# Five edits to the order of loads, sums and banks in a two-layer fp32 decoder kernel on one core

## The chip, the core and the metric

The kernel runs on one core of a Trainium2 chip. The metric is the device time of one launch in microseconds. Five engines work side by side, each with its own queue of instructions: TensorE (PE in the profile: matmuls and transposes), VectorE (DVE), ScalarE (ACT), GpSimd (POOL) and SyncE (SP), which in this kernel issues every DMA. Each engine takes its instructions in order, each as soon as what it waits for has come. One launch computes the whole trunk.

## The reference

The input x has 1024 rows of 1024 floats. Two layers each do

```
h = h + 0.5 * rmsnorm(swiglu(rmsnorm(h)))      first feed-forward, inner width 1408
h = h + rmsnorm(mixer(rmsnorm(h)))             layer 0: differential + gated linear attention
                                               layer 1: stick-breaking attention, 8 heads
h = h + 0.5 * rmsnorm(swiglu(rmsnorm(h)))      second feed-forward
```

with `swiglu(x) = (silu(x @ wg) * (x @ wu)) @ wd`. The mixers project their input (`hyb_w_in`, `sb_w_qkv`), attend causally and project back (`hyb_w_out`, `sb_w_out`). Everything is float32.

## The kernel before

**Products.** A float32 product is three matmuls in a faster format: each operand is split into a high and a low part, and `mm3` (L281 to L283) adds high·high, high·low and low·high into one PSUM bank. The high part is a copy on ScalarE (tile `hl` L271, for weights `wq` L330), the low part a subtraction on VectorE (L272, L331). So each operand, raw or summed, passes through ScalarE and VectorE before TensorE can use it. On top of that, large products are computed with fewer block products by sums and differences of blocks: the inputs' on VectorE (`combos`), the weights' on GpSimd (`rawt`/`t` L424 to L427 and `t` L64).

**Feed-forward.** `gu` has two phases over 11 column tiles c. Phase 1 multiplies the first half of the rows (A) with the gate weights (`pa`). In phase 1, after tile 2, `second_half()` transposes the other half of the rows (`xps` L321, copied to `xr` L323), and on tiles 3 to 6 `combos` builds the block sums that phase 2 needs, on VectorE. Phase 2 makes for each tile five quarter products into three banks: `pb`, `pc`, `pd`, then `pc` and `pd` once more, which are drained in between by adds on VectorE (L433, L436, L438). Then comes the down product: `da`, `db`, `dc`, `de`, and `dd` in two parts; between the parts of `dd` the epilogue adds to h, norms the first half of the rows and `make_x` (L250) transposes it for the next stage (`xps` L257).

**make_x** takes for the mixer a second output: a scaled copy of each transposed tile on ScalarE into `rawx`, and four DMAs that store these to `xkeep` in HBM.

**Mixer inputs.** `values()` (L738) computes the value rows by block products: `va`; then `vb` with the weights b21; then, after the second half's norm and transposes (`make_raw`, `xr`), `vc`, and on the same banks the products on S2, S1, S3, S4. The weight sums t1, t2, t4 (`T`, twelve operations, L64) and t3 are GpSimd's. The input differences are VectorE's: L800 to L802 for S2 and S1, L832 for S4. They need the raw first-half input K, which is loaded back from `xkeep` (four loads of `xk`).

**Heads.** `heads()` runs through units (head, block of 128 queries) in a pipeline; `start` is called on a head's first unit, `fill` on its fourth, and gives steps (the next head's projection, or `out_steps` in the last head) of which one is done per unit. In the stick-breaking mixer a unit's scores go through ScalarE (L1000, L1001), GpSimd (masks, L1004) and VectorE (a scan L1007, a product L1010) back to TensorE (`tps`). `out_weights` makes one of four sets of block sums of the output weights (loads, four GpSimd subtractions, four stores to `wsum`), at a head's start: in layer 1 one set for each of heads 0 to 3, in layer 0 two for each of heads 0 and 1. Before the last head the score pools are closed and opened again with two score banks and not four, so that `out_steps`, seven steps over four banks `oa`, has banks.

**What sets the order.** A scheduler takes the code and decides the order on each engine, with pools of buffers as limits: `raw` (name `rp`, four buffers, for everything that is loaded raw), `w`, `hl`, and eight PSUM banks. All loads and stores stand in SP's queue in one order, so a store that waits for GpSimd holds up each load behind it.

Of the kernel before, what the change touches and what calls it, by code (L numbers as in the profile page):

```python
# [87 lines left out]
class Trunk:  # L88
# [161 lines left out]
    def make_x(self, xns, gname, gi, pool, keep=None):  # L250

        nc = self.nc
        res = []
        for k in range(KD):
            ps = self.tp.tile([P, TB], F32, name="xps", tag="tp")
            for t in range(NTT):
                nc.tensor.transpose(ps[:, t * P:(t + 1) * P], xns[t][:, k * P:(k + 1) * P], self.ident)  # L257
# [86 lines left out]
    def gu(self, cx, wg, wu, A, xn1, gname, gi):  # L344
# [51 lines left out]
        for c in range(NF):  # L396
            h = [self.ph.tile([P, TB], F32, name="ph%d" % tb, tag="ph") for tb in range(2)]
            r = self.load_w(wg, c)
            w0, w1 = self.split_w(r[:, 0:4]), self.split_w(r[:, 4:8])
            ps = self.acc.tile([P, TB], F32, name="pa", tag="acc")  # L400
            self.quarter(ps, w0, A[0:4], True, True)
            nc.scalar.copy(out=h[1], in_=ps)
            if second:
                a12()
            second.append((ps, w1, h))
            ph.append(h)
            if c == 2:
                second_half()
            if 3 <= c <= 6:
                combos(c - 3)  # L410
# [7 lines left out]
        for c in range(NF):  # L418
# [11 lines left out]
            pd = self.acc.tile([P, TB], F32, name="pd", tag="acc")  # L430
            u2 = h[1]
            self.quarter(pb, self.split_w(t2), S[2], True, True)
# [5 lines left out]
            tt(out=c22, in0=pd, in1=c22, op=ALU.add)  # L438
            w4, w3 = self.split_w(b21), self.split_w(b22)
            self.quarter(pc, w4, A22, False, True)  # L440
            c21 = tm.tile([P, TB], F32, name="c21", tag="c21")
            tt(out=c21, in0=pc, in1=u2, op=ALU.add)
            nc.scalar.activation(out=c21, in_=c21, func=AF.Silu)
            self.quarter(pd, w3, S[4], False, True)
            c12 = tm.tile([P, TB], F32, name="c12", tag="c12")
            tt(out=c12, in0=pd, in1=u2, op=ALU.add)
# [143 lines left out]
    def down_strassen(self, w, ph, pg, hsrc, hdst, nxt):  # L590
# [127 lines left out]
        nxt0 = self.make_x(xns, *nxt, self.xp, self.xk if nxt[0] == "mix_pre_g" else None) if nxt else None  # L718
# [21 lines left out]
    def values(self, l, w, cols, X, xn1, vd):  # L740
# [25 lines left out]
        for t in range(NTT):  # L766
            nc.scalar.copy(out=p1[t], in_=pa[t])
        T = []
# [4 lines left out]
        self.rows_product(pb, A[4:8], weights(B.b21), True, 2)  # L773
# [5 lines left out]
        sp, kp = self.dyn(cv, "sx", 5), self.dyn(cv, "xk", KD // 2)  # L779
        kt = [kp.tile([P, 2, TB], F32, name="xk", tag="xk") for _ in range(KD // 2)]  # L780
        for k in range(KD // 2):
            nc.sync.dma_start(out=kt[k].rearrange("p k t -> p (k t)"), in_=self.xk[:, 2 * k * TB:2 * (k + 1) * TB])
        K = [kt[k // 2][:, k % 2] for k in range(KD)]
# [168 lines left out]
    def heads(self, H, first, second, third, fill, start):  # L952

        LAG = 2
        n = H * NQ
        pend, steps, last = [], [], None
        for u in range(n + LAG + 1):
# [24 lines left out]
            if old:  # L984
                last = old[:2] + (second(*old),)
            if done:
                third(*done)
        for step in steps:
            step()
# [23 lines left out]
    def sb_mixer(self, X):  # L1013
        a, nc = self.a, self.nc
        w = a["sb_w_qkv"][0]
        with ExitStack() as cx:
# [19 lines left out]
            def start(h):  # L1036
                if h == 7:
                    pd.close()
                    self.mctx.close()
                    self.open_mix(pd, 2, 1, 1)  # L1040
                if h % 2 and h < 7:
                    v[h // 2 + 1] = self.load_v(vp, self.vd, (h + 1) * P)
                if h < 4:
                    self.out_weights(1, h)

            def second(h, i, atts):
# [7 lines left out]
                if i == NQ - 1:  # L1054
# [3 lines left out]
                       lambda h: project(h + 1) if h < 7 else self.out_steps(1), start)  # L1058
# [195 lines left out]
    def hyb_mixer(self, X):  # L1254
# [3 lines left out]
        with ExitStack() as cx:  # L1258
# [81 lines left out]
            with ExitStack() as cd:  # L1340
# [9 lines left out]
                def start(h):  # L1350
                    if h == 3:
                        pd.close()
                        self.mctx.close()
                        self.open_mix(pd, 2, 1, 1)
                    if h == 1:
                        v[1] = self.load_v(vp, self.vd, 256)
                    if h < 2:
                        self.out_weights(0, 2 * h)
                        self.out_weights(0, 2 * h + 1)
# [10 lines left out]
                def fill(h):  # L1370
                    if h == 3:
# [5 lines left out]
                           third, fill, start)  # L1377
                pd.close()

    def put_o(self, l, k, ot, last=False):  # L1380
# [7 lines left out]
        if j >= 0:  # L1388
# [5 lines left out]
            self.out_sums(r, x, ot)  # L1394
            self.nc.sync.dma_start(out=self.sd[j][:, :S], in_=r)
            self.nc.sync.dma_start(out=self.sd[j][:, S:], in_=x)
# [19 lines left out]
    def out_weights(self, l, j):  # L1416
# [6 lines left out]
        B.sub(t[:, 0], r[:, 1], r[:, 0])  # L1423
        B.sub(t[:, 1], b[:, 1], r[:, 1])
        B.sub(r[:, 0], b[:, 1], t[:, 0])
        B.sub(b[:, 0], b[:, 0], r[:, 0])
        for i, src in ((0, t[:, 0]), (2, t[:, 1]), (1, r[:, 0]), (3, b[:, 0])):
            self.nc.sync.dma_start(out=self.td[j][:, i * TB:(i + 1) * TB], in_=src)

    def out_steps(self, l):  # L1430
# [10 lines left out]
        def step(n):  # L1441
            if n == 0:
                st["p1"] = halves([pair("p1") for _ in range(2)])
                st["c11"] = halves([pair("c11") for _ in range(2)])
                st["accs"] = self.new_accs("oa")
# [3 lines left out]
            a, b = self.split(r[:, 0], self.hp), self.split(r[:, 1], wp)  # L1449
            for t in range(NTT):  # L1450
                ts = slice(t * P, (t + 1) * P)
                self.mm3(st["accs"][t], a[:, 0, ts], a[:, 1, ts], b[:, 0], b[:, 1], n == 0, n in (3, 6), more=n > 3)
            if n in (3, 6):
                for t in range(NTT):
                    nc.scalar.copy(out=st["p1" if n == 3 else "c11"][t], in_=st["accs"][t])

        self.begun = B, order, st
        return [lambda n=n: step(n) for n in range(7)]
# [100 lines left out]
    def build(self):  # L1559
# [3 lines left out]
        self.xk = self.dram.tile([P, KD * TB], F32, name="xkeep")  # L1563
# [54 lines left out]
```

## Time and profile before

| | us |
|---|---|
| median of three runs | 2564.71 (2562.7 to 2566.6) |
| profiled execution, its own time | 2561.61 |
| its span | 2559.9 |
| TensorE busy | 2376.2 |
| VectorE busy | 1862.8 |
| ScalarE busy | 1173.6 |
| GpSimd busy | 945.3 |

The mean granted TensorE clock is 0.969 of full speed. TensorE's share is 93%; the rest is many short waits, the longest of 14 us, and after some of them the granted clock stands at half speed for a while. In the rows of the timeline the columns are start, duration, engine, line, operation, written tile<-read tiles, shapes and count, and in brackets the idle time before and what ended it. In the rows of the waits: who waited for what, total, times, longest. In the rows of windows: the window, its length, each engine's busy time with its number of instructions, the granted clock, the share of the DMA engines and GB/s.

### The profile page before, as it was taken

The page shows a single profiled execution, that of the slowest core. Times are in us where ns is not written, and L with a number is a line of the kernel's source. Part 1 is how long each engine was busy: PE and PEld are TensorE (multiplying, and loading weights), DVE is VectorE, ACT ScalarE, POOL GpSimd, SP SyncE. Part 2 cuts the span into 40 slices and gives each one's busy share as a digit, 9 for nine tenths or more (in the row PEclk, how much of TensorE's full clock was granted, in tenths as well). Part 3 has the DMA queues.
Part 4 walks back from the last instruction along what each step waited for, and adds up shares of the span by engine and source line. Part 5 has one row for each costly group of instructions (what it writes and reads, how often), then busy time and mean ns, then how long its engine had stood idle before and what let it go on. Part 6 is the DMA issues. An engine that isn't in the chain of part 4 may idle for free. (4 is left out here: it accounts for less than half of the span.)

```text
span 2559.9 us, 32090 instructions
## 1 busy us (share of the span) xinstructions
PE 2376.2 (93%) x11229; PEld 1937.5 (76%) x11229; DVE 1862.8 (73%) x2778; ACT 1173.6 (46%) x2335; POOL 945.3 (37%) x804
## 2 busy tenths in 40 slices
PE   7999977998999898999989999779899999899998
PEld 6887856777777777787868878558788887678876
DVE  6768866387577777767888678665676778686788
ACT  6423545332466667323465234444333345752343
POOL 2545423113211241555424454241332334234553
PEclk9999988999999999999999999889899999999999
DMA  5223554514311564223552225465321135622255
GB/s 162 82 80 97 179 179 159 173 46 136 115 58 58 169 201 124 83 75 115 165 185 83 83 70 198 157 205 163 125 83 58 50 120 166 192 83 71 73 157 197
DMA packets 272073, 318.49 MB, mean 124 GB/s; under 512 B 13780, under 2 KB 190120, under 8 KB 271912
## 3 DMA queue, kind: packets, MB, share of 16 engines
q1 hardware_dynamic: 271912, 316.45, 39.0%
q8 instruction: 88, 1.44, 0.2%
q14 instruction: 73, 0.60, 0.1%
HBM read 254.54 MB, written 61.87 MB: 124 GB/s over the span
## 5 line engine op out<-in xcount | busy, mean ns | idle before, releaser
L330 ACT CAST wq<-rawt 128x512 fp32r<-128x512 f32 x264 | 163.1, 623 | 355.5 <-PE pc L283 170.2
L225 POOL TENSOR_TENSOR rs<-ms,nhalf 128x1 f32<-128x1 f32 (+1 forms) x136 | 100.6, 745 | 427.4 <-DVE ms L223 374.3
L331 DVE TENSOR_TENSOR wq<-rawt,wq 128x512 fp32r<-128x512 f32 x264 | 239.2, 912 | 25.8 <-ACT wq L330 18.5
L424 POOL TENSOR_TENSOR rawt<-rawt 128x512 f32<-128x512 f32 x44 | 82.7, 1879 | 379.3 <-DMA rawt<-in_ffn_w_up_dram 136.8
L272 DVE TENSOR_TENSOR hl<-rawd,hl 128x512 fp32r<-128x512 f32 x168 | 150.8, 899 | 84.2 <-ACT hl L271 83.5
L281 PE MATMUL pps<-hl,wh 128*128 128x512 f32 x512 | 208.4, 407 | 0.0
L283 PE MATMUL pps<-hl,wl 128*128 128x512 f32 x512 | 202.5, 396 | 1.5 <-DVE wl L858 1.5
L282 PE MATMUL pps<-hl,wh 128*128 128x512 f32 x512 | 202.9, 396 | 0.0
L271 ACT CAST hl<-rawd 128x512 fp32r<-128x512 f32 x168 | 103.4, 619 | 186.6 <-PE dc L283 33.2
L281 PE MATMUL pd<-hl,wq 128*128 128x512 f32 x352 | 138.9, 395 | 10.7 <-DVE c L438 10.7
L281 PE MATMUL pc<-hl,wq 128*128 128x512 f32 x352 | 137.8, 392 | 6.6 <-DVE c L436 3.4
L281 PE MATMUL pa<-hl,wq 128*128 128x512 f32 x352 | 141.0, 401 | 3.1 <-DVE hl L275 3.1
L283 PE MATMUL pa<-hl,wq 128*128 128x512 f32 x352 | 139.8, 398 | 3.5 <-DVE wq L331 3.5
L282 PE MATMUL pa<-hl,wq 128*128 128x512 f32 x352 | 140.3, 399 | 0.0
L282 PE MATMUL pd<-hl,wq 128*128 128x512 f32 x352 | 138.8, 394 | 0.0
L283 PE MATMUL pd<-hl,wq 128*128 128x512 f32 x352 | 138.6, 394 | 0.0
L283 PE MATMUL pc<-hl,wq 128*128 128x512 f32 x352 | 138.3, 393 | 0.0
L282 PE MATMUL pc<-hl,wq 128*128 128x512 f32 x352 | 138.3, 393 | 0.0
L272 DVE TENSOR_TENSOR hl<-ph,hl 128x512 fp32r<-128x512 f32 x136 | 131.5, 981 | 0.0
L929 PE MATMUL z<-k,q 128*128 128x512 f32 (+2 forms) x480 | 124.3, 379 | 5.6 <-ACT e L1082 2.5
L1007 DVE TENSOR_TENSOR_SCAN a<-a,zero 128x128 f32<-128x128 f32 (+3 forms) x64 | 93.9, 1467 | 47.0 <-POOL a L1004 46.8
L283 PEld LDWEIGHTS pps<-hl,wl 128*128 128x128 f32 x512 | 96.6, 189 | 22.0 <-DVE wl L858 2.3
(343 smaller groups left out, 6885.5 us busy)
## 6 DMA issues: line engine op xcount, KB each, us to landing
rawt<-in_ffn_w_gate_dram SPq DMA_DIRECT2D x88, 512.0 KB, 4.0
rawd<-in_ffn_w_down_dram SPq DMA_DIRECT2D x60, 512.0 KB, 3.8
rawd<-in_ffn_w_down_dram SPq DMA_DIRECT2D x116, 256.0 KB, 2.8
rawt<-in_ffn_w_up_dram SPq DMA_DIRECT2D x44, 512.0 KB, 4.0
hres<-h SPq DMA_DIRECT2D x40, 512.0 KB, 2.9
h<-hres SPq DMA_DIRECT2D x40, 512.0 KB, 4.6
rawd<-in_hyb_w_in_dram SPq DMA_DIRECT2D x36, 256.0 KB, 3.5
rawd<-in_sb_w_qkv_dram SPq DMA_DIRECT2D x36, 256.0 KB, 3.5
```

The costliest lines, as they stand in the source:

```text
L225: nc.gpsimd.tensor_tensor(out=rs, in0=ms, in1=self.nhalf.to_broadcast([P, n]) if n > 1 else self.nhalf, op=ALU.pow)
L271: nc.scalar.copy(out=t[:, 0], in_=src)
L272: nc.vector.tensor_tensor(out=t[:, 1], in0=src, in1=t[:, 0].bitcast(F32), op=ALU.subtract)
L281: nc.tensor.matmul(ps, lhsT=ah, rhs=bh, start=first, stop=False, skip_group_check=more)
L282: nc.tensor.matmul(ps, lhsT=ah, rhs=bl, start=False, stop=False, skip_group_check=more)
L283: nc.tensor.matmul(ps, lhsT=al, rhs=bh, start=False, stop=last, skip_group_check=more)
L330: nc.scalar.copy(out=w[:, 0], in_=src)
L331: nc.vector.tensor_tensor(out=w[:, 1], in0=src, in1=w[:, 0].bitcast(F32), op=ALU.subtract)
L424: gt(out=b11, in0=b12, in1=b11, op=ALU.subtract)
L929: nc.tensor.matmul(z[:, :wide], lhsT=lhs[:, i * P:(i + 1) * P], rhs=rhs[:, c0:c0 + wide], start=j == 0, stop=j == len(passes) - 1 and not ...
L1007: nc.vector.tensor_tensor_scan(out=ra, data0=ra, data1=self.zero1.to_broadcast([P, n]), initial=1.0, op0=ALU.mult, op1=ALU.add)
```

## The change

Five things change.

1. `make_x` makes no raw copies and no stores. `values()` makes the raw inputs K itself, by eight additions of high and low part on GpSimd. In `values()` the weights b21 are loaded and split ahead of GpSimd's sums T.
2. In `gu`, `second_half()` comes after tile 3 and the combinations on tiles 4 to 7.
3. For the last tile of phase 2 the fourth and fifth quarter products have banks of their own, `pe` and `pf`.
4. `out_weights` and the sums of finished heads load first and put their GpSimd sums and stores into a list that runs one unit later. `out_weights` is called on unit 6 of heads 0 to 3 in layer 1, and on units 1 and 6 of heads 0 and 1 in layer 0.
5. The score pools keep four banks in the last head. `out_steps` takes two banks for two row tiles at a time: eight steps, four for each pair of row tiles; the operands are loaded and split in the first four and kept.

```diff
-    def make_x(self, xns, gname, gi, pool, keep=None):
+    def make_x(self, xns, gname, gi, pool):
...
-            if keep is not None:
-                if k % 2 == 0:
-                    r = self.rp.tile([P, 2, TB], F32, name="rawx", tag="raw")
-                nc.scalar.activation(out=r[:, k % 2], in_=ps, func=AF.Copy, scale=self.col(gname, gi * KD + k))
-                if k % 2:
-                    nc.sync.dma_start(out=keep[:, (k - 1) * TB:(k + 1) * TB], in_=r.rearrange("p k t -> p (k t)"))
...
-            if c == 2:
+            if c == 3:
                 second_half()
-            if 3 <= c <= 6:
-                combos(c - 3)
+            if 4 <= c <= 7:
+                combos(c - 4)
...
+            if last:
+                self.quarter(pe, self.split_w(b21), A22, True, True)
+                self.quarter(pf, self.split_w(b22), S[4], True, True)
+                tt(out=c12, in0=pd, in1=u2, op=ALU.add)
+                tt(out=c21, in0=pe, in1=c22, op=ALU.add)
+                tt(out=c22, in0=pd, in1=c22, op=ALU.add)
+                nc.scalar.activation(out=c21, in_=c21, func=AF.Silu)
+                tt(out=c12, in0=pf, in1=c12, op=ALU.add)
...
+        W = weights(B.b21)
         T = []
...
-        self.rows_product(pb, A[4:8], weights(B.b21), True, 2)
+        self.rows_product(pb, A[4:8], W, True, 2)
...
-        for k in range(KD // 2):
-            nc.sync.dma_start(out=kt[k].rearrange("p k t -> p (k t)"), in_=self.xk[:, 2 * k * TB:2 * (k + 1) * TB])
+        for k in range(KD):
+            gt(out=K[k], in0=A[k][:, 0].bitcast(F32), in1=A[k][:, 1].bitcast(F32), op=ALU.add)
...
+            soon, self.soon = self.soon, []
+            for f in soon:
+                f()
+            if u < n:
+                weights(h, i)
...
-                if h == 7:
-                    pd.close()
-                    self.mctx.close()
-                    self.open_mix(pd, 2, 1, 1)
...
-                if h < 4:
-                    self.out_weights(1, h)
...
+                       lambda h, i: self.out_weights(1, h) if h < 4 and i == 6 else None)
...
+                def weights(h, i):
+                    if h < 2 and i in (1, 6):
+                        self.out_weights(0, 2 * h + (i == 6))
...
+        self.soon.append(sums)
...
-        return [lambda n=n: step(n) for n in range(7)]
+        return [lambda tp=tp, ns=ns: step(tp, ns) for tp in range(2) for ns in ((0, 1), (2, 3), (4, 5), (6,))]
```

How the order moves is shown at three places of layer 0. The first is TensorE's queue between the two parts of `dd`, before (L257 is make_x's transpose, `fo_...` the normed row tiles, L281 to L283 the three matmuls of a product):

```order
L283 MATMUL dd_2642<-hl 128x512
L257 MATMUL xps<-ident,fo_1965 128x128 x4
L257 MATMUL xps<-ident,fo_1966 128x128 x4
L257 MATMUL xps<-ident,fo_1967 128x128 x4
L257 MATMUL xps<-ident,fo_1968 128x128 x4
L257 MATMUL xps<-ident,fo_1965 128x128
```

and after (here L256 is the transpose and L274 to L276 are the three matmuls):

```order
L274 MATMUL dd_2642<-hl 128x512
L256 MATMUL xps<-ident,fo_1967 128x128 x4
L274 MATMUL dd_2643<-hl 128x512
L275 MATMUL dd_2641<-hl 128x512
L276 MATMUL dd_2641<-hl 128x512
L274 MATMUL dd_2641<-hl 128x512
L256 MATMUL xps<-ident,fo_1968 128x128 x4
L275 MATMUL dd_2642<-hl 128x512
```

Before, 28 of the 32 transposes stand in one run ahead of the second part of `dd`; after, its matmuls stand between them. The second place is GpSimd's queue in `values()`, before:

```order
L64 TENSOR_TENSOR t_3349<-rawd 128x512
L64 TENSOR_TENSOR t_3350<-rawd,t_3349 128x512
L64 TENSOR_TENSOR t_3351<-rawd,t_3350 128x512
L64 TENSOR_TENSOR rawd<-rawd 128x512 x4
L819 TENSOR_TENSOR c_3777<-c_3777,p_3593 128x512
```

and after:

```order
L64 TENSOR_TENSOR t_3355<-rawd 128x512
L64 TENSOR_TENSOR t_3356<-rawd,t_3355 128x512
L64 TENSOR_TENSOR t_3357<-rawd,t_3356 128x512
L790 TENSOR_TENSOR xk<-hl 128x512 x8
L64 TENSOR_TENSOR rawd<-rawd 128x512 x4
```

The eight additions that make K stand behind the last of the twelve sums T and ahead of the sums t3. The third place is VectorE's queue behind `vb`, before (the numbered `t_...` are low halves of weight sums, `xr` of the second half's inputs, L800 the first difference with K):

```order
L775 TENSOR_TENSOR vo<-vb_3364,p_3308 128x512
L272 TENSOR_TENSOR hl<-t_3326,hl 128x512
L272 TENSOR_TENSOR hl<-xr,hl 128x512 x5
L800 TENSOR_TENSOR xk<-xk,xr 128x512
L272 TENSOR_TENSOR hl<-xr,hl 128x512
L801 TENSOR_TENSOR xr<-xr 128x512
```

and after (L265 are the low halves here, L807 the first difference with K):

```order
L783 TENSOR_TENSOR vo<-vb_3370,p_3294 128x512
L807 TENSOR_TENSOR xk<-xk,xr 128x512
L265 TENSOR_TENSOR hl<-t_3345,hl 128x512
L265 TENSOR_TENSOR hl<-xr,hl 128x512
L265 TENSOR_TENSOR hl<-t_3357,hl 128x512
L265 TENSOR_TENSOR hl<-xr,hl 128x512
```

The first difference with K (L807) now stands ahead of two of the four low halves that `vc` needs (`t_3345`, `t_3357`).

More of the change, by code (lines that the diff above doesn't have):

```diff
@@ L430, in gu @@
             pd = self.acc.tile([P, TB], F32, name="pd", tag="acc")
+            if c == NF - 1:
+                pe = self.acc.tile([P, TB], F32, name="pe", tag="acc")
+                pf = self.acc.tile([P, TB], F32, name="pf", tag="acc")
             u2 = h[1]
+            last = c == NF - 1
             self.quarter(pb, self.split_w(t2), S[2], True, True)
@@ L778, in values @@
         self.foctx.close()
[L779 to L783 removed]
+        sp, kp = self.dyn(cv, "sx", 5), self.dyn(cv, "xk", KD)
+        K = [kp.tile([P, TB], F32, name="xk", tag="xk") for k in range(KD)]
+        for k in range(KD):
+            gt(out=K[k], in0=A[k][:, 0].bitcast(F32), in1=A[k][:, 1].bitcast(F32), op=ALU.add)
         H = [None] * KD
@@ L950, in transposer, with heads @@
         return res, [lambda j0=j0: group(j0) for j0 in range(0, i + 1, 4)]
-    def heads(self, H, first, second, third, fill, start):
+    def heads(self, H, first, second, third, fill, start, weights):
         LAG = 2
@@ L987, in heads @@
                 third(*done)
-        for step in steps:
+        for step in steps + self.soon:
             step()
@@ L1393, in put_o, with sums @@
                 self.nc.sync.dma_start(out=ot, in_=self.ot[l][k])
-            self.out_sums(r, x, ot)
-            self.nc.sync.dma_start(out=self.sd[j][:, :S], in_=r)
-            self.nc.sync.dma_start(out=self.sd[j][:, S:], in_=x)
+            def sums():
+                self.out_sums(r, x, ot)
+                self.nc.sync.dma_start(out=self.sd[j][:, :S], in_=r)
+                self.nc.sync.dma_start(out=self.sd[j][:, S:], in_=x)
+            self.soon.append(sums)
     def out_order(self, l):
@@ L1421, in out_weights, with sums @@
         b = B.load((j + 4, 0), (j + 4, 1))
[L1423 to L1428, printed above, removed]
+        def sums():
+            B.sub(t[:, 0], r[:, 1], r[:, 0])
+            B.sub(t[:, 1], b[:, 1], r[:, 1])
+            B.sub(r[:, 0], b[:, 1], t[:, 0])
+            B.sub(b[:, 0], b[:, 0], r[:, 0])
+            for i, src in ((0, t[:, 0]), (2, t[:, 1]), (1, r[:, 0]), (3, b[:, 0])):
+                self.nc.sync.dma_start(out=self.td[j][:, i * TB:(i + 1) * TB], in_=src)
+        self.soon.append(sums)
     def out_steps(self, l):
@@ L1439, in out_steps, with load @@
         st = {}
-        def step(n):
+        ab = []
+        def load(n):
             if n == 0:
@@ L1448, in step @@
             nc.sync.dma_start(out=r[:, 1], in_=B.src(n, 0))
[L1449 to L1455, printed above, removed]
+            ab.append((self.split(r[:, 0], self.hp), self.split(r[:, 1], wp if n % 2 else self.xp)))
+        def step(tp, ns):
+            if 0 in ns:
+                st["accs"] = [self.acc.tile([P, TB], F32, name="oa%d" % t, tag="acc") for t in range(2)]
+            for n in ns:
+                if tp == 0:
+                    load(n)
+                a, b = ab[n]
+                for i in range(2):
+                    t = 2 * tp + i
+                    ts = slice(t * P, (t + 1) * P)
+                    self.mm3(st["accs"][i], a[:, 0, ts], a[:, 1, ts], b[:, 0], b[:, 1], n == 0, n in (3, 6),
+                             more=n > 3)
+                if n in (3, 6):
+                    for i in range(2):
+                        nc.scalar.copy(out=st["p1" if n == 3 else "c11"][2 * tp + i], in_=st["accs"][i])
         self.begun = B, order, st
-        return [lambda n=n: step(n) for n in range(7)]
+        return [lambda tp=tp, ns=ns: step(tp, ns) for tp in range(2) for ns in ((0, 1), (2, 3), (4, 5), (6,))]
     def mix_out(self, l, hsrc, hdst, gname, gi):
```

31 lines of the change are left out of this document (12 added, 19 removed).

## The prediction

> **What bounds the kernel now.** I read the page's busy times first, then the waits of TensorE, then the timeline around each long wait. TensorE is the bound:
>
> ```profile
> PE 2376.2 (93%) x11229; PEld 1937.5 (76%) x11229; DVE 1862.8 (73%) x2778; ACT 1173.6 (46%) x2335; POOL 945.3 (37%) x804
> PEclk9999988999999999999999999889899999999999
> ```
>
> The change takes no matmul out, so it can only win from TensorE's idle time (2559.9 - 2376.2 = 184 us, the modelled ends counted in) and from stretches where the granted clock is low. The waits of TensorE say where the idle time lies:
>
> ```profile
> PE vb L281 <- ACT hl L271: 27.3, 2, 14.0
> PE xps L257 <- DVE ms L223: 15.1, 9, 6.4
> PE dd L281 <- ACT hl L271: 14.0, 4, 6.6
> PE tps L945 <- DVE b L1010: 11.1, 1, 11.1
> PE pd L281 <- DVE c L438: 10.7, 4, 2.7
> PE xps L321 <- ACT fo L237: 9.9, 5, 2.3
> PE pc L281 <- DVE c L436: 3.4, 2, 1.7
> ```
>
> Each row is a place that one part of the change touches. The columns are total, times, longest. For every place the question is what comes late next once the wait is gone.
>
> **Part 1, the raw input tiles (make_x).** Before, the eight scaled copies into rawx and their four stores to xkeep stand in SP's queue ahead of the loads for dd's second product, and in TensorE's order all but four of the transposes stand ahead of that product. The change removes copies and stores, and the order then mixes that product with the transposes. The trace holds the same code without the stores: the end of layer 0's second feed-forward. The windows run from the last matmul ahead of the gap to the last of dd, over 106 matmuls each:
>
> ```profile
> core 0: us, PE busy (x) PEld busy (x) DVE busy (x) ACT busy (x) POOL busy (x), PEclk, DMA share, GB/s
> 333.60:377.30 43.70, 27.52 (x106) 20.07 (x105) 24.22 (x43) 23.72 (x45) 10.04 (x11) 0.73 0.50 169
> 1288.10:1313.60 25.50, 21.84 (x106) 16.36 (x106) 22.84 (x41) 16.92 (x35) 5.44 (x5) 1.00 0.66 207
> 1630.40:1673.60 43.20, 27.89 (x106) 20.40 (x105) 24.54 (x43) 23.70 (x45) 10.09 (x11) 0.72 0.50 171
> ```
>
> Same matmuls, 25.5 us at clock 1.00 against 43.7 and 43.2 at 0.73 and 0.72: a gain of 18.2 + 17.7 = **36 us** (30 to 38, since in the mixer the norm that follows may hold va a little).
>
> **Part 2, values().** The wait ahead of vb goes, because b21 is now loaded ahead of Pool's sums. The raw inputs K are now made by eight adds on Pool, behind its twelve weight sums T. The rows of layer 0:
>
> ```profile
> 402.64 0.79 PE L281 MATMUL vb<-hl 128*128 128x512 f32 x1 [13.36 <-ACT hl L271]
> 423.59 0.50 PE L281 MATMUL vc<-hl 128*128 128x512 f32 x1 [2.15 <-ACT hl L271]
> 389.00 1.27 POOL L64 TENSOR_TENSOR t<-rawd 128x512 f32<-128x512 f32 x1
> 402.38 2.95 POOL L64 TENSOR_TENSOR t<-rawd,t 128x512 f32<-128x512 f32 x2
> 402.62 1.58 DVE L272 TENSOR_TENSOR hl<-rawd,hl 128x512 fp32r<-128x512 f32 x1 [11.80 <-ACT hl L271]
> 389.07 1.75 DVE L239 TENSOR_SCALAR xn<-h,rs 128x1024 f32<-128x1024 f32 x1 [0.66 <-POOL rs L225]
> 426.58 0.68 DVE L800 TENSOR_TENSOR xk<-xk,xr 128x512 f32<-128x512 f32 x1
> 440.46 2.49 DVE L272 TENSOR_TENSOR hl<-xr,hl 128x512 fp32r<-128x512 f32 x4
> rawd<-in_hyb_w_in_dram SPq DMA_DIRECT2D x36, 256.0 KB, 3.5
> ```
>
> Count from dd's end (377.3). After vc (48 matmuls, 10.9 us) comes the product on S2, which ends at +68.3 before (423.59 + 2 x 11.0), with every product after it back to back. So the question is when S2 ends, not when vb starts. In the changed kernel the four raw buffers that b21 takes come free only when DVE has made its low halves, and in DVE's order those stand behind the last xn, which ends at 390.8, +13.5. Four splits of 0.7 us bring +16.3, the next load 3.5 us: +19.8. Pool's twelve sums take 405.3 - 389.0 = 16.3: +36.1. The first K is there at about +37.6. From the first xk (426.58) to the splits of the row at 440.46 (end 443.0) DVE takes 16.4 us, and the last quarter of the product 2.7: S2 ends at +56.7, 11.6 us earlier, if nothing disturbs. But K1 to K7 now run beside that very chain:
>
> ```profile
> 1034.60 1.78 DVE L331 TENSOR_TENSOR wq<-t,wq 128x512 fp32r<-128x512 f32 x1
> 1048.05 0.67 DVE L331 TENSOR_TENSOR wq<-rawt,wq 128x512 fp32r<-128x512 f32 x1
> 1034.09 1.75 POOL L424 TENSOR_TENSOR rawt<-rawt 128x512 f32<-128x512 f32 x1
> 1022.66 7.05 POOL L424 TENSOR_TENSOR rawt<-rawt 128x512 f32<-128x512 f32 x1 [29.93 <-DVE s L376]
> ```
>
> A DVE operation that meets one of Pool takes 1.78 us and not 0.67: 1.1 us for each Pool operation. Eight adds cost DVE 8.8, so S2 ends at +65.5: **3 us earlier in each layer**, 6 in all. The ends are 11.6 earlier (no meeting) and 10 later (all 20 Pool operations met: 22 us).
>
> The Trainium skill (SBUF — State Buffer, "SBUF: two separate sides") says that DVE with two SBUF inputs and a reading GpSimd operation share a port pair as an exclusive lock: whichever starts first holds it for its whole instruction. By that rule an add of 1.75 us could hold up DVE by all of it, 14 us per layer and S2 at +70.7, 2.4 later than before; the trace agrees that the two take turns.
>
> **Part 3, second_half a tile later, combos on 4 to 7.** In second feed-forwards TensorE waits for xps L321 because the norm is late. With a tile more ahead those gaps (9.9 us in all) close. But the transposed inputs come no earlier there, and in first feed-forwards, where nothing waited, they come a tile later. Behind them stands DVE's chain to the first add of phase 2:
>
> ```profile
> 44.40:96.20 51.80, 51.80 (x229) 42.80 (x228) 47.81 (x70) 32.88 (x60) 18.09 (x8) 1.00 0.29 82
> 997.40:1049.40 52.00, 50.37 (x222) 41.26 (x220) 47.04 (x69) 32.44 (x60) 18.15 (x8) 1.00 0.29 81
> 95.52 0.68 DVE L436 TENSOR_TENSOR c<-pc,ph 128x512 f32<-128x512 f32 x1
> 96.70 0.39 PE L281 MATMUL pc<-hl,wq 128*128 128x512 f32 x1
> 1049.48 0.47 PE L281 MATMUL pc<-hl,wq 128*128 128x512 f32 x1 [1.70 <-DVE c L436]
> ```
>
> From the first combination to that add it takes 51.8 and 52.0 us, with DVE busy over 90%. TensorE gives 229 matmuls 51.8 us, so a tile of 24 is 5.4. Begun 5.4 later, with 0.5 us of slack at 96.70, the add is 4.9 late, less what DVE squeezes out of its 4.0 idle: 1 to 5 us in each first feed-forward. I take 4 with the clock after it. In the second ones what closes ahead opens at pc. Sum: **8 us lost** (0 to 14).
>
> **Part 4, own banks for the last gate/up tile.** TensorE no longer waits for c L438, since pe and pf need no bank of pc and pd: 10.7 us in four waits. What is late next, DVE's splits for the down product, falls into work of pe and pf that is there anyway. Behind the second gap the clock is low, behind the first it is not:
>
> ```profile
> 1193.78 0.47 PE L281 MATMUL pd<-hl,wq 128*128 128x512 f32 x1 [2.69 <-DVE c L438]
> 1194.90:1198.10 3.20, 3.20 (x9) 2.53 (x8) 3.20 (x4) 0.46 (x1) 2.48 (x2) 0.50 0.32 82
> 240.90:243.90 3.00, 2.99 (x13) 2.48 (x14) 3.00 (x3) 0.00 (x0) 2.28 (x3) 1.00 0.26 85
> ```
>
> A window at 0.50 costs half of its 3.2 us. I count two such, one in each layer's second feed-forward: 10.7 + 2 x 1.6 = 13.9, less some slack at pc: **13 gained** (10 to 15). The Trainium skill (TensorE: Matmul & The Clock Gate, "What's actually happening") has the clock fall after an idle window of about 3.4 us; by it these gaps would cost no clock and the gain were 10.7. The row at 0.50 behind a gap of 2.69 disagrees.
>
> **Part 5, head 0 of layer 1.** Pool's output-weight sums move to unit 6 and one unit on:
>
> ```profile
> 1798.73 1.66 SPq L1428 DMA_DIRECT2D wsum<-rawd  x2
> 1800.48 1.13 SPq L849 DMA_DIRECT2D rawt<-in_sb_w_qkv_dram  x2
> 1805.04 1.04 ACT L857 CAST wh<-rawt 128x1024 fp32r<-128x1024 f32 x1 [9.21 <-DMA rawt<-in_sb_w_qkv_dram]
> 1810.09 0.48 PE L945 MATMUL tps<-ident,b 128*128 128x128 f32 x1 [11.14 <-DVE b L1010]
> ```
>
> The head's activations queue on ACT behind the cast at 1805.04, that behind a load, and that on SP behind stores that wait for Pool. From cast to tps is 5.05 us, which stays, less what ran earlier: some 4. So 11.1 - 4 = 7 go, and 2 of low clock: **9 gained**. But the order of the changed kernel still has two sets of sums ahead of the head's masks, so the ends are 13 gained and 3 lost.
>
> **Part 6, the last heads.** Four score banks stay open, and the output product comes in eight steps of two banks, its splits all in the first four:
>
> ```profile
> 840.00:900.00 60.00, 50.93 (x266) 40.46 (x266) 44.91 (x101) 40.02 (x109) 13.59 (x14) 0.91 0.58 189
> 2095.00:2125.00 30.00, 26.85 (x145) 23.13 (x144) 27.05 (x36) 18.63 (x38) 9.66 (x13) 0.94 0.68 228
> ```
>
> 9.1 and 3.2 us are idle there. I take **3 gained**: at most all 12, or 8 lost where DVE (44.91 of 60 busy) gets its splits in half the steps.
>
> **Sum.** -36 - 6 + 8 - 13 - 9 - 3 = -59. The profiled execution took 2561.6 us, so 2502.6; the median of the runs is 3.1 above it: **2506**. The terms' ends alone make 2490 to 2522.
>
> **Rivals.**
> - *No wait takes a lost one's place* (20%). Pool and DVE do not meet in values() (11.6 and not 3 per layer: -17) and the late add of part 3 is hidden (-8): 2481. DVE's 4.0 idle us in the chain speak for it, the doubled rows against.
> - *Pool and DVE take turns* (25%). All of Pool's 20 operations in values() meet DVE: +10 and not -3 per layer, +26: 2532. The saturated rows above speak for it; but DVE is idle for stretches while T is summed (the 11.80 above). Beside it stands the lock of the Trainium skill (SBUF — State Buffer, "SBUF: two separate sides"), which bears out that both lose.
> - *Head 0 still waits* (11%), since the sums are ordered ahead of the masks as before: the change doesn't do there what it says. +9: 2515.
> - *Slower* (4%). DVE starves Pool, as in the 7.05 us row, through the sums that S2 waits for: 12 T and 4 K. At 7.05 us they end at 19.8 + 16 x 7.05 = +133, S2 about 6 later, 70 per layer above before: 2506 + 2 x 73 = 2652. It decides from the point where 59 us are eaten, S2 at +95, so an add of some 4.3 us. Against it: even at 1034.09, beside busy DVE, an add took 1.75.
>
> **How the numbers follow.** The forecast has 40%. Its range, 2490 to 2522, holds the third rival too; reaching out to the first and second with some us around them gives 2474 to 2537, with the slower case and the tails left out. A difference of 0.2% (5 us) is what a measurement here can tell from no change. All cases but the last lie below 2559: faster 0.95, same 0.01, slower 0.04.
>
> **What would show it.** Right: the matmuls of dd and xps in about 26 us at clock 1.00; no vb wait, but a wait of the S2 product or vc on DVE; a pc wait of some 4 us in first feed-forwards; no wait on c L438; the wait at tps under 5. Wrong: long waits at va or at dd that part 1 should have taken, S2 before +60 or after +75, Pool adds over 3 us, or a new wait in the last heads.

## The result and the profile after

The changed kernel takes 2524.57 us (median of four runs, 2522.18 to 2525.91) against 2563.70 for the kernel before in the same runs: a ratio of 0.985 (95% interval 0.983 to 0.987). It is 39 us faster; 59 were forecast, and the range reached from 2474 to 2537. The rows that answer to the page's first and second part:

```profile
PE 2376.5 (94%) x11229; PEld 1930.8 (76%) x11229; DVE 1875.0 (74%) x2782; ACT 1158.0 (46%) x2319; POOL 994.7 (39%) x820
PEclk9999998999999999999999999989999999999999
```

TensorE's work is the same 2376 us. GpSimd has 16 operations and 49 us more; the sixteen additions of K take 25 of these (12.63 us for eight in each layer), and the rest is that others of its operations take longer. Eight rows of the waits of TensorE after the change:

```profile
PE vc L275 <- DVE hl L265: 8.6, 4, 2.4
PE tps L952 <- DVE b L1024: 8.0, 1, 8.0
PE dc L274 <- DVE c L704: 7.7, 3, 2.8
PE xps L314 <- ACT fo L237: 5.7, 3, 2.4
PE va L274 <- ACT hl L264: 5.7, 3, 2.9
PE pa L274 <- ACT ph L395: 5.3, 2, 2.7
PE va L276 <- DVE hl L265: 5.1, 2, 2.6
PE xps L256 <- DVE ms L223: 2.8, 9, 0.5
```

Of before, the waits at vb (up to 14.0 us), at xps (up to 6.4) and at dd on the weights (up to 6.6) and those on the last tile's sum are gone. New or longer are `vc` and `va`, `dc` and `pa`: all on VectorE or ScalarE. Where the time came from shows when the span is cut at the first matmul of each stage (first `pa`, `pb`, `pc`, `da`, `dd`, `va`, `vc`, `pps`, `z`, `oa`, `od` of each half layer, read from the two timelines). The sum of the cuts is the difference of the spans, 35.7 us:

| stretch, summed over its places | measured | forecast |
|---|---|---|
| `dd` to `va`, twice (part 1) | -18.5 - 17.2 = -35.8 | -36 |
| `va` to `pps`, twice (part 2) | +3.8 + 4.5 = +8.3 | -6 |
| `pa` to `pc`, four times (part 3) | -1.5 + 1.1 + 0.9 + 1.3 = +1.8 | +8 |
| `pc` to `dd`, four times (part 4) | +3.2 - 4.0 + 2.4 - 5.6 = -4.0 | -13 |
| layer 1, `z` to `oa` (part 5) | -3.2 | -9 |
| layer 0 `z` to `od`, layer 1 `oa` to `od` (part 6) | -0.2 + 2.4 = +2.2 | -3 |
| the rest | -5.0 | 0 |

Part 1 as the windows show it, from the 106th (108th in layer 0) matmul ahead of the end of `dd`:

```profile
335.20:360.80 25.60, 22.11 (x108) 16.56 (x107) 23.05 (x41) 17.07 (x35) 5.19 (x5) 1.00 0.52 165
1613.40:1639.30 25.90, 21.70 (x106) 16.44 (x106) 23.36 (x41) 17.12 (x35) 5.26 (x5) 1.00 0.54 163
```

25.6 and 25.9 us at full clock, where 43.7 and 43.2 stood and the forecast took 25.5 from its control. SP's queue shows one reason, the six loads for the second part of `dd`. Before, they stand in one row, directly behind three stores to `xkeep` (from 346.86); after, they come in two rows and far earlier:

```profile
351.10 9.94 SPq L613 DMA_DIRECT2D rawd<-in_ffn_w_down_dram  x6
313.33 13.62 SPq L620 DMA_DIRECT2D rawd<-in_ffn_w_down_dram  x4
335.10 1.21 SPq L620 DMA_DIRECT2D rawd<-in_ffn_w_down_dram  x2
```

No run below puts only the copies and stores back, so what the freed queue gains and what the other order of the transposes gains are not parted.

### The profile page after: what moved, and what is told of

It reads as the page before. It is cut to its first block, busy times and chain, and to the rows that moved or that the text cites. A ratio compares the mean times of both kernels' runs of the same rounds, so it can differ in the third digit from the quotient of the medians.

```text
span 2524.2 us, 32090 instructions
## 1 busy us (share of the span) xinstructions
PE 2376.5 (94%) x11229; PEld 1930.8 (76%) x11229; DVE 1875.0 (74%) x2782; ACT 1158.0 (46%) x2319; POOL 994.7 (39%) x820
## 5 line engine op out<-in xcount | busy, mean ns | idle before, releaser
L417 POOL TENSOR_TENSOR rawt<-rawt 128x512 f32<-128x512 f32 x44 | 92.1, 2093 | 371.7 <-DMA rawt<-in_ffn_w_up_dram 207.4
L274 PE MATMUL pps<-hl,wh 128*128 128x512 f32 x512 | 208.3, 407 | 0.0
L276 PE MATMUL pps<-hl,wl 128*128 128x512 f32 x512 | 202.6, 396 | 2.3 <-DVE wl L865 2.3
L265 DVE TENSOR_TENSOR hl<-rawd,hl 128x512 fp32r<-128x512 f32 x168 | 142.1, 848 | 21.3 <-ACT hl L264 21.0
L274 PE MATMUL pa<-hl,wq 128*128 128x512 f32 x352 | 141.7, 403 | 7.7 <-ACT ph L395 5.3
L276 PE MATMUL pa<-hl,wq 128*128 128x512 f32 x352 | 138.7, 397 | 2.9 <-DVE wq L324 2.6
L265 DVE TENSOR_TENSOR hl<-ph,hl 128x512 fp32r<-128x512 f32 x136 | 135.2, 1006 | 0.0
L274 PE MATMUL pc<-hl,wq 128*128 128x512 f32 x336 | 131.3, 391 | 2.8 <-DVE c L433 2.8
L276 PE MATMUL pc<-hl,wq 128*128 128x512 f32 x336 | 132.1, 393 | 0.0
L275 PE MATMUL pc<-hl,wq 128*128 128x512 f32 x336 | 132.1, 393 | 0.0
L275 PE MATMUL pd<-hl,wq 128*128 128x512 f32 x336 | 131.3, 391 | 0.0
L276 PE MATMUL pd<-hl,wq 128*128 128x512 f32 x336 | 131.2, 390 | 0.0
L274 PE MATMUL pd<-hl,wq 128*128 128x512 f32 x336 | 131.0, 390 | 0.0
L276 PEld LDWEIGHTS pps<-hl,wl 128*128 128x128 f32 x512 | 96.8, 189 | 23.3 <-DVE wl L865 3.6
```

The costliest lines, as they stand in the source:

```text
L265: nc.vector.tensor_tensor(out=t[:, 1], in0=src, in1=t[:, 0].bitcast(F32), op=ALU.subtract)
L274: nc.tensor.matmul(ps, lhsT=ah, rhs=bh, start=first, stop=False, skip_group_check=more)
L275: nc.tensor.matmul(ps, lhsT=ah, rhs=bl, start=False, stop=False, skip_group_check=more)
L276: nc.tensor.matmul(ps, lhsT=al, rhs=bh, start=False, stop=last, skip_group_check=more)
L417: gt(out=b11, in0=b12, in1=b11, op=ALU.subtract)
```

## The experiments

**K without GpSimd's additions.** The edit, in `values()`:

```diff
-        for k in range(KD):
-            gt(out=K[k], in0=A[k][:, 0].bitcast(F32), in1=A[k][:, 1].bitcast(F32), op=ALU.add)
...
-            tt(out=K[j], in0=K[j], in1=R[j], op=ALU.subtract)
+            tt(out=K[j], in0=A[j][:, 0].bitcast(F32), in1=R[j], op=ALU.subtract)
+            tt(out=K[j], in0=K[j], in1=A[j][:, 1].bitcast(F32), op=ALU.add)
```

and the same for `K[j + 4]`.

> The changed kernel without the eight additions of K on GpSimd: VectorE takes the second half's input from the high and the low part directly, two subtractions or additions where there was one (8 more operations of 0.6 us per layer on VectorE). In the changed kernel values() takes 104.7 and 104.4 us from the first va to the first pps (before: 101.0 and 99.9), and VectorE's operations beside the additions take 1.75 us and not 0.68. Theory: the additions, queued behind the sums T and slowing VectorE, hold the S2 chain; then values() falls by 10 to 15 us in each layer, to about 92, and the whole to about 2500. Rival: the sums T themselves, or the second half's norm, hold vc and S2; then values() stays above 100 us and the whole at 2520 to 2530, since VectorE gets 4.8 us more work per layer.

Measured: 2514.15 us, ratio 0.981 (0.978 to 0.983); `va` to `pps` 97.2 and 97.5 us. The theory holds in kind: 7.5 and 6.9 us went in the two layers, not 10 to 15. The timelines of VectorE and GpSimd, of the changed kernel and then of this one:

```profile
398.70 12.63 POOL L790 TENSOR_TENSOR xk<-hl 128x512 f32<-128x512 f32 x8
411.30 6.76 POOL L64 TENSOR_TENSOR rawd<-rawd 128x512 f32<-128x512 f32 x4
400.04 1.77 DVE L807 TENSOR_TENSOR xk<-xk,xr 128x512 f32<-128x512 f32 x1 [3.22 <-POOL xk L790]
416.86 1.75 DVE L265 TENSOR_TENSOR hl<-t,hl 128x512 fp32r<-128x512 f32 x1
418.53 0.68 DVE L265 TENSOR_TENSOR hl<-xr,hl 128x512 fp32r<-128x512 f32 x1
429.37 2.48 DVE L265 TENSOR_TENSOR hl<-xr,hl 128x512 fp32r<-128x512 f32 x4
```

```profile
396.21 1.19 DVE L805 TENSOR_TENSOR xk<-hl,xr 128x512 f32<-128x512 f32 x1
404.12 1.78 DVE L806 TENSOR_TENSOR xk<-xk,hl 128x512 f32<-128x512 f32 x1
405.82 0.68 DVE L807 TENSOR_TENSOR xr<-xr 128x512 f32<-128x512 f32 x1
421.62 2.50 DVE L265 TENSOR_TENSOR hl<-xr,hl 128x512 fp32r<-128x512 f32 x4
```

In the changed kernel VectorE takes 1.75 us for each operation as long as GpSimd runs (to 418), then 0.68. Without the additions the slow stretch, beside the t3 sums alone, ends at 405.8. Counted from the first `va` (360.67 and 359.92), the chain's last splits start 7.0 us earlier, with eight more operations in the layer.

**The additions run, but nobody waits for them.** The kernel above with

```diff
+        spare = kp.tile([P, TB], F32, name="spare", tag="spare", bufs=1)
+        for k in range(KD):
+            gt(out=spare, in0=A[k][:, 0].bitcast(F32), in1=A[k][:, 1].bitcast(F32), op=ALU.add)
```

> The kernel with K's differences on VectorE from the high and low parts, and beside it the eight additions of high and low part on GpSimd all the same, into a spare tile that nobody reads. This parts the two costs of the additions: nobody waits for them, but they still run beside VectorE's chain. Without the additions values() took 97.2 and 97.5 us, with them in their old role 104.7 and 104.4. Theory: the slowing of VectorE (1.75 for 0.68 us, some 1.1 us for each addition it meets) is the larger part; values() is 102 to 106 us. Rival: the queue behind T is the larger part; then values() stays at 97 to 100 us.

Measured: 2531.74 us, ratio 0.988 (0.986 to 0.990); `va` to `pps` 106.3 in both layers. That is just above the theory's 102 to 106; the rival's 97 to 100 is out. Against the kernel above, 97.2 and 97.5, it is 9.1 and 8.8 us for eight additions whose result is never read: 1.1 us each, by slowing VectorE.

```profile
399.46 6.83 POOL L791 TENSOR_TENSOR spare<-hl 128x512 f32<-128x512 f32 x4
405.07 1.77 DVE L809 TENSOR_TENSOR xk<-xk,hl 128x512 f32<-128x512 f32 x1
418.49 1.76 DVE L810 TENSOR_TENSOR xr<-xr 128x512 f32<-128x512 f32 x1
411.90 0.62 ACT L264 CAST hl<-xr 128x512 fp32r<-128x512 f32 x1 [7.58 <-DVE xr L811]
412.57 0.79 PE L274 MATMUL va<-hl 128*128 128x512 f32 x1 [4.24 <-ACT hl L264]
```

VectorE again takes 1.76 us for an operation, until the one begun at 418.49 is done, and TensorE waits 4.24 at `va`, for a cast that had waited for VectorE's chain. The t3 sums come later too, but nothing waits for them here. The two engines start an operation every 1.7 us each, by turns. This is what the Trainium skill (SBUF — State Buffer, "SBUF: two separate sides") calls an exclusive lock on a shared port pair: the loser blocks until the other's whole instruction is done. The trace agrees on the turns; a pair takes 1.7 us, somewhat less than the two alone one after the other (0.60 and 1.27).

**b21 behind the sums again.** `W = weights(B.b21)` goes back behind the loop of T.

> The changed kernel with the loads of b21 behind the weight sums T again; K stays on GpSimd. Theory: S2, which waits for K behind T, sets the end of values(), so the wait ahead of vb comes back and T is ready earlier; the two cancel, values() stays within 3 us of 104.7 and 104.4 and the whole within 5 us of 2525. Rival: the earlier vb is worth its 13 us in each layer; then values() takes 115 us or more and the whole 2540 or more.

Measured: 2532.78 us, ratio 0.988 (0.985 to 0.991); `va` to `pps` 108.8 and 109.0, 4.0 and 4.5 more than in the changed kernel. The wait ahead of `vb` is back, at 12.6 us where 13.4 stood before:

```profile
388.22 0.80 PE L274 MATMUL vb<-hl 128*128 128x512 f32 x1 [12.64 <-ACT hl L264]
```

So a wait of 12.6 us, with a clock of 0.50 behind it (388.0 to 392.0), is worth 4 us per layer. In exchange the sums T, whose end K waits for, are done 31.0 us after the first `va` and not 38.1. The truth lies between theory (within 3) and rival (10 or more), nearer to the theory.

**The last tile on the old banks.** `last = False` in `gu`.

> The changed kernel with the last gate/up tile on the banks pc and pd as before. In the changed kernel the waits on c L438 (10.7 us) are gone, but the stretch from da to dd grew by 6.1, 3.2, 5.8 and 0.4 us, with new waits of dc on VectorE. Theory: VectorE sets the pace in the down product, so the gain is handed back there; without the banks da to dd shrinks again and the whole is only 3 to 6 us slower, about 2529. Rival: the waits at dc come from another part, and the banks gain what was forecast; then the whole is 12 to 14 us slower, about 2538, and da to dd stays long.

Measured: 2527.50 us, ratio 0.986 (0.984 to 0.989), 2.9 us above the changed kernel, about the theory's 3 to 6 and within the spread of both; the rival's 2538 is out. `da` to `dd`, in the changed kernel and then without the banks:

```profile
239.70:321.90 82.20, 78.37 (x337) 64.04 (x336) 61.77 (x82) 37.41 (x74) 43.17 (x29) 0.98 0.57 182
```

```profile
242.10:318.20 76.10, 76.10 (x337) 63.05 (x336) 67.11 (x76) 37.24 (x74) 39.30 (x27) 1.00 0.60 194
```

TensorE is busy for all 76.1 us without the banks, and idle for 3.8 of 82.2 with them, the clock a little lower. The 10.7 us of waits on the sum come back without the banks, and in part go to `dc` with them (7.7 us). Over the four stretches from `pc` to `dd` the sum is 923.0 us without the banks and 922.1 before the change; the changed kernel and the seven runs of this section with its down product have 914.5 to 921.5.

**Own banks for the second part of dc as well.**

```diff
-        product(pc, A(0, 1), lambda j: half(j + KH, 1), False, more=last_k(0, 1))
+        pf = new("df")
+        product(pf, A(0, 1), lambda j: half(j + KH, 1), True, more=last_k(0, 1))
...
-            tt(out=c, in0=pc[t], in1=u2[t], op=ALU.add)
+            tt(out=c, in0=pf[t], in1=c22[t], op=ALU.add)
```

> The changed kernel, and in the down product the second part of dc gets four banks of its own (df) and is added to c22 (which holds the first part and u2), so that it need not wait for VectorE to drain the first part. Theory: with the banks pe and pf TensorE reaches the down product 4 us earlier while VectorE does not, and the 2.8 us waits on c L704 and the clock after them hand the gain back; freed of that bank, da to dd falls from 82.2, 79.4, 82.0 us by 3 to 5 us each and the whole by 8 to 12, to 2513 to 2517. Rival: VectorE is saturated there, and the next low half is late in place of the drain; then da to dd falls by under 2 us and the whole stays at 2521 to 2525.

Measured: 2520.14 us, ratio 0.983 (0.981 to 0.986). `da` to `dd` falls to 77.9, 77.4 and 77.9 us, by 4.3, 2.0 and 4.1, as the theory has it; but the stretch behind, from `dd` on, grows by 3.8, 3.0 and 2.6, as the rival has it one stage later:

```profile
322.41 0.50 PE L274 MATMUL dd<-hl 128*128 128x512 f32 x1 [2.07 <-DVE fo L709]
```

The wait has moved from `dc` to `dd`, which uses the banks that VectorE now drains last. So 1 us was left over in these stretches, and 4.4 in the medians, of which the spread may hold a part.

**second_half and the combinations as before.** Tile 2, and tiles 3 to 6.

> The changed kernel with second_half after tile 2 and the combinations on tiles 3 to 6 as before. Theory, as forecast but smaller: the later place gains nothing in total (by the stretches from pa to da it looks like 0 to 3 us), so the whole is 2521 to 2528. Rivals: the forecast's 8 us lost, then 2517; or a gain of the 9.9 us of xps waits, then 2535.

Measured: 2526.06 us, ratio 0.986 (0.984 to 0.988): 1.5 us above the changed kernel, no difference that can be told. The theory holds.

**The output weights' sets as before.** Sets at the heads' first units, sums at once.

> The changed kernel with the output weights' sets at the heads' first units again and all sums at once, not a unit later. Theory: two sets are ordered ahead of the first masks in either case; the wait at tps of layer 1's head 0 returns from 8.0 to about 11 us, and the whole is 2526 to 2532. Rival: the moved sets gain nothing, and the 3 us come from other work in front; then the wait stays near 8 us and the whole at 2525 or below.

Measured: 2531.02 us, ratio 0.988 (0.985 to 0.991). The wait at `tps` of layer 1's head 0 is longer than either theory had it:

```profile
1787.23 0.47 PE L952 MATMUL tps<-ident,b 128*128 128x128 f32 x1 [15.50 <-DVE b L1024]
```

But this wait is not steady: in kernels that do not differ there it was 8.0 (changed), 11.2 (K on VectorE) and 3.0 us (old banks). It has two parts: how late ScalarE's cast behind the raw load comes, counted from the head's first `z`, and the time from the cast to `tps`. The cast comes 10.0 us after `z` before the change, 9.5 in this run, 1.7 in the changed kernel, and between 0.0 and 1.7 in the other runs of this section with the sets moved, none held, and K made by GpSimd. With K on VectorE, or on VectorE beside the spare additions, it is 4.8 to 6.2, and why stays open. So the move of the sets brings the load forward. The second part is taken up under part 5.

The move is worth some 6 us in the medians, and not all of it lies in layer 1: from `pps` to `z` of layer 0 this run takes 207.8 us, the kernel before 206.1, the changed kernel 203.2. TensorE's waits there on VectorE's `zq` go from 7.1 to 4.4 us and back to 7.3.

**Every set held until its head has a first block.** In layer 1, ahead of each load of a set:

```diff
+        if gate is not None:
+            for i in range(2):
+                self.t.nc.gpsimd.tensor_copy(out=r[:, i, 0:1], in_=gate)
```

> The changed kernel, but in layer 1 each set of output-weight sums first waits for the first block of its head's output (four copies of one column on GpSimd per set), so that no set can be ordered ahead of the first masks. Theory: what is left of the wait at tps in head 0 (8.0 us) is GpSimd's second set standing ahead of the masks; the wait falls to 4 or 5 us, the table load and the chain through GpSimd and VectorE, and the whole by 3 to 5 us to about 2521. Rival: the wait is ScalarE's late cast behind a load of raw weights; then it stays at 7 to 9 us and the whole at 2525.

Measured: 2531.79 us, ratio 0.988 (0.986 to 0.991): 7 us slower than the changed kernel, which neither theory nor rival had. The wait in head 0 is down to 3.5 us and on another operation, and others stand in its place:

```profile
1785.93 0.44 PE L955 MATMUL tps<-ident,b 128*128 128x128 f32 x1 [3.50 <-DVE att L957]
1829.17 1.22 PE L1063 MATMUL po<-att,v 128*128 128x128 f32 x8 [3.34 <-DVE att L957]
```

and in its waits

```profile
PE po L1063 <- DVE att L957: 8.6, 5, 3.3
```

A set's sums now stand between masks: VectorE's scan at 1822.90 waits 5.0 us for a mask behind them, and TensorE behind VectorE. How much of the loss is theirs, and how much that of the gate's own copies, was not parted; the last kernel below, with one set held, has no such wait at `po`.

**Seven output steps, two score banks.** The last head as before.

> The changed kernel with the last head as before: score pools closed and opened with two banks, seven output steps over four banks. Theory: the half-width steps gain nothing in layer 0 and lose 2 to 3 us in layer 1 (a wait of 4.1 us ahead of oa); the whole is 2521 to 2525. Rival, as forecast: they gain 3 us or more, and the whole is 2528 or above.

Measured: 2520.98 us, ratio 0.984 (0.982 to 0.986), 3.6 us below the changed kernel. Its profile has `oa` to `od` 1.2 and 1.9 us shorter in the two layers, but `da` to `dd` of layer 0's first feed-forward, which the edit does not touch, is 2.6 us shorter too. The theory's 2521 to 2525 holds, the rival's 2528 is out. All profiles together tell more. From `oa` to `od`, ten of the eleven with eight steps take 76.0 to 76.8 us in layer 0 (the changed kernel 78.7), those with seven 77.4 to 79.0; in layer 1 it is 80.8 to 83.7 against 79.1 to 79.8. The half-width steps gain 1 to 3 us in layer 0 and lose 1 to 5 in layer 1.

**The gains together.** K on VectorE and the banks for `dc`; the same with seven steps; and the first of the two with the second set of layer 1 alone held.

> The changed kernel with K's differences on VectorE and the four own banks for the second part of dc. If the two gains add up (10.4 us in the first, 4.4 in the second against the changed kernel), the whole is 2508 to 2512; if VectorE, which is now the next limit in both places, takes the second one back, 2512 to 2516.

> The kernel before this one, and the last head with two score banks and seven output steps over four banks as before. The half-width steps cost 3.6 us in the changed kernel; if that holds here, this one is 2 to 5 us faster than the one before it; if the difference was the spread of the down product's waits from run to run, the two are within 2 us.

> K's differences on VectorE and own banks for dc, and in layer 1 only the second set of output-weight sums held until the first block of head 0 is done; sets one, three and four as in the changed kernel. With all four held, the wait at tps of head 0 went from 8.0 to 3.5 us, but three new waits of 2.2 to 3.3 us at po came with the other sets. If the second set alone is what holds head 0, the 10.8 us wait of the kernel without the hold falls to 3 to 6 us and one wait of up to 3.3 comes: 2503 to 2508. If the casts behind the raw loads set it, the wait stays at 8 to 11 and the whole is 2508 or above.

Measured: 2508.77 us, ratio 0.979 (0.977 to 0.981); 2510.14, ratio 0.979 (0.977 to 0.981); 2505.29, ratio 0.977 (0.976 to 0.979). The first two gains add up. The half-width steps make no difference in the medians here (in the profiles 1.5 us gained in layer 0, 3.5 lost in layer 1), so part of the 3.6 us above was spread. Holding the second set alone shortens the wait in head 0 from 10.76 to 6.79 us, the two profiles' rows:

```profile
1756.39 0.47 PE L953 MATMUL tps<-ident,b 128*128 128x128 f32 x1 [10.76 <-DVE b L1025]
```

```profile
1757.01 0.47 PE L956 MATMUL tps<-ident,b 128*128 128x128 f32 x1 [6.79 <-DVE b L1028]
1752.45 1.04 ACT L868 CAST wh<-rawt 128x1024 fp32r<-128x1024 f32 x1 [6.57 <-DMA rawt<-in_sb_w_qkv_dram]
```

The first mask shows that the set's sums were the cause, without the hold and with it:

```profile
1755.03 0.29 POOL L1019 TENSOR_SCALAR_AFFINE_SELECT a<-a 128x128 f32<-128x128 f32 x1
1755.65 0.29 POOL L1022 TENSOR_SCALAR_AFFINE_SELECT a<-a 128x128 f32<-128x128 f32 x1 [18.98 <-ACT a L1018]
```

Without the hold it stands behind the sums, 5 us after ScalarE's first activation (1750.02); with it, it follows the activation (1755.31) at once. From the cast to `tps` it is 9.2 us without and 4.6 with. What is left hangs on ScalarE's cast behind a raw load, which ends 3.5 us ahead of `tps`. So both expectations were half right. The fastest kernel is 3.5 us below the one without the hold, at intervals that overlap.

## Why the forecast was right, and where it was not

**Part 1** was right in place, mechanism and size. The control of the same code in the same trace gave 25.5 us, and 25.6 and 25.9 came. In all the runs above with the down product's banks as in the changed kernel or before it, `dd` to `va` takes 38.6 to 39.4 us, where 57.3 and 56.7 stood. It is the whole of the net gain in the profiles.

**Part 2** had the right mechanism and the wrong sign of the sum: 3 us gained per layer were forecast, 3.8 and 4.5 were lost. TensorE's waits in layer 0, where the additions run:

```profile
403.53 0.50 PE L275 MATMUL vc<-hl 128*128 128x512 f32 x1 [2.13 <-DVE hl L265]
406.89 0.79 PE L275 MATMUL vc<-hl 128*128 128x512 f32 x1 [2.38 <-DVE hl L265]
415.96 0.50 PE L274 MATMUL va<-hl 128*128 128x512 f32 x1 [2.12 <-ACT hl L264]
419.26 0.79 PE L276 MATMUL va<-hl 128*128 128x512 f32 x1 [2.57 <-DVE hl L265]
```

K0 came at +39.2 (400.0, with `dd`'s end at 360.8; forecast +37.6). The step that failed is "eight adds cost DVE 8.8, so S2 ends at +65.5". GpSimd goes straight from K to the four t3 sums, so 11 of VectorE's operations ran at 1.75 and not 8: start to start 1.68 and not 0.60, 11 x 1.08 = 11.9. And 33 operations stand between the first `xk` and the splits' end, 27 before, since low halves for `vc` had moved in among them: 6 x 0.60 = 3.6. From 400.0 to 431.9 the chain took 31.8 us where 16.4 + 8.8 = 25.2 were reckoned; with the later K, S2's product ends at +72 (the products on S2 and S1 end together at 443.8, and one takes 10.9), and not at +65.5 (before: +68.3). These ends are reckoned: S2's and S1's products share their banks, TensorE's last wait is the one that ends at 419.26, and the chain's end, 39.2 + 31.8 + 2.7 = 73.7, would be 1.6 later than what came. The price of one meeting, 1.1 us, was right; the runs with and without the spare additions give 9 us for eight. The mistake was to show an instruction order and not to count it through. The rule that adds could cost VectorE their whole 1.75 us is not borne out: 1.1 were lost for each.

**Part 3** was too dark: 8 us lost were forecast, about 2 are in the stretches and none in the medians. The transposed inputs came 2.2 us later in the first feed-forward and not 5.4, and VectorE drew its chain together:

```profile
46.58 0.69 DVE L369 TENSOR_TENSOR s<-xr 128x512 f32<-128x512 f32 x1 [3.79 <-ACT xr L316]
95.72 0.68 DVE L433 TENSOR_TENSOR c<-pc,ph 128x512 f32<-128x512 f32 x1
96.54 0.47 PE L274 MATMUL pc<-hl,wq 128*128 128x512 f32 x1 [0.87 <-DVE c L433]
1018.65 0.52 PE L274 MATMUL pa<-hl,wq 128*128 128x512 f32 x1 [2.66 <-ACT ph L395]
```

The chain from the first combination to the add took 49.8 us, not 51.8. TensorE waited 0.87 us at `pc` here, and 1.91 in layer 1's first feed-forward, where up to 4.9 had been reckoned. In second feed-forwards the xps waits fell from 9.9 to 5.7 us, and the `pc` waits of before (1.7 in each) went too: a wait of 2.66 at `pa` opened in each, on ScalarE's copy of the phase 1 sums. The step "what closes ahead opens at pc" had the wrong place; the stretches grew by 1.1 and 1.3 us all the same. With `second_half` and the combinations at their old places the waits are 11.0 at xps and 1.7 at each `pc` again.

**Part 4** was right that the waits on the sum go, and wrong in one step: "what is late next, DVE's splits for the down product, falls into work of pe and pf". The splits and drains of the down product on VectorE came no earlier. TensorE stood at the first bank it wanted back:

```profile
298.54 0.68 DVE L265 TENSOR_TENSOR hl<-rawd,hl 128x512 fp32r<-128x512 f32 x1
299.14 0.68 DVE L265 TENSOR_TENSOR hl<-ph,hl 128x512 fp32r<-128x512 f32 x1
299.75 0.68 DVE L265 TENSOR_TENSOR hl<-rawd,hl 128x512 fp32r<-128x512 f32 x1
300.35 2.47 DVE L704 TENSOR_TENSOR c<-dc,u 128x512 f32<-128x512 f32 x4
301.18 0.47 PE L274 MATMUL dc<-hl 128*128 128x512 f32 x1 [2.74 <-DVE c L704]
```

`dc`'s matmuls were done at 298.44; the drain that would free it stood behind three splits. Given other banks, TensorE waits at `dd` (the runs above). So the 13 us are 3 to 4: in this stretch VectorE sets the pace once TensorE gains 4 us on it. In the changed kernel both second feed-forwards keep a gain (4.0 and 5.6 us) and both first ones lose. Only layer 1's second one, with no next stage to prepare, keeps it in all eight profiles with this down product (225.1 to 227.4 us against 230.7 before; layer 0's second one 228.3 to 232.0 against 232.3); that the missing next stage is the reason was not tested.

**Part 5** had the place right and the size too large: 3.2 us in the profile, against 9, and by its own sign, a wait at `tps` under 5, it did not come true: 8.0. The step that failed is "from cast to tps is 5.05 us, which stays". The cast, the second set's first sums, the first mask and `tps`:

```profile
1767.02 1.05 ACT L864 CAST wh<-rawt 128x1024 fp32r<-128x1024 f32 x1 [5.41 <-DMA rawt<-in_sb_w_qkv_dram]
1770.22 2.48 POOL L64 TENSOR_TENSOR rawt<-rawd 128x512 f32<-128x512 f32 x2 [18.30 <-DMA rawd<-in_sb_w_out_dram]
1775.22 0.29 POOL L1018 TENSOR_SCALAR_AFFINE_SELECT a<-a 128x128 f32<-128x128 f32 x1
1776.58 0.48 PE L952 MATMUL tps<-ident,b 128*128 128x128 f32 x1 [7.97 <-DVE b L1024]
```

The cast came some 8 us earlier than before, counted from the head's first `z`; but the second set's sums now fall between it and the masks, as the third rival said, and from cast to `tps` it is 9.6 us and not 5.05. Together they take 3.8 us off the time from `z` to `tps`. Holding that set brought the 9.2 us of its kernel back to 4.6. In runs that do not differ there the wait moves with the cast, between 2.6 and 11.9 us; the loads that the cast waits for stand on SP behind stores of value rows and sums, and why they come later with K on VectorE stays open.

**Part 6** gained nothing that can be told: 2.2 us lost by the profile, 3.6 by one comparison, none by another. The forecast took one sum for both layers; by the profiles layer 0 gains and layer 1 loses, as said above.

The forecast of 2506 was 19 us too low: 14 in part 2, 9 in part 4, 6 in part 5, 5 in part 6, against 6 in part 3 and 5 gained elsewhere, and some 4 from the profiled execution's place among its runs. Of the 5, 2.9 lie in layer 0 from `pps` to `z`; the run with the sets as before gives them back, so they come from the sets and sums that were moved in layer 0, for which the forecast had no term. That the total came within 19 us is so in part luck: 34 us of too much gain stand against 15 that were not reckoned or reckoned too dark. The measured time lies outside 2490 to 2522, which the forecast gives as the terms' ends, and inside the range only because that reaches out to the rivals. Nor do the ends make 2490 to 2522: added up as they stand in the parts, they reach from 2464 to 2570. Of the rivals, the second (Pool and DVE take turns, 2532) came nearest in mechanism, and the third (head 0 still waits) was right about its place.

## What to carry to other kernels

A wait that goes is worth what the next queue behind it allows: reckon the chain of the other engine, in operations counted in the new order, before the wait is priced. An addition on an idle engine is not free when it takes turns with the busy one on operands in SBUF; here eight of them cost 9 us, and doing the same work with more operations on the busy engine was faster. The gain that could be read off a control in the same trace, the same code without the step, was the one that came true to the microsecond.

## What had not been expected of the hardware

GpSimd and VectorE, both adding or subtracting 128x512 fp32 tiles, went strictly by turns: each started one operation every 1.7 us, where VectorE alone starts one every 0.60 us and GpSimd alone takes 1.27. Both lose, VectorE 1.1 us for each GpSimd operation, and an operation of which nobody reads the result costs as much as any other.
